# Feed-forward in three blocks of 768 tokens, its split weight operands all made during the sweeps; projection weights split once

## The chip, the cores and the metric

The kernel runs on one core of a Trainium2 chip. The metric is the device time of one launch in microseconds. A core has five engines that run side by side and meet at semaphores: TensorE (PE, with its weight loads as PEld), VectorE (DVE), ScalarE (ACT), GpSimd (POOL), and SyncE (SP), which issues most of the DMA transfers. Each engine takes its instructions strictly in the order in which they stand in its queue.

## The reference, cut to what matters

There are 2304 tokens (2048 of `x_sample`, 256 of `x_prompt`), each a vector of 1024 numbers, and one layer.

```
h = rmsnorm(x, norm1_g);  p = h @ w_in                      # 1024 -> 2336
a_out = gla_mixer(q, k, v, g, lr, ...)                      # gated linear attention, both directions
b_out = spatial_gating(gelu(u), gelu(vs), ...)              # 128 x 128 mixing of positions
c_out = pool_mixer(xp, ...)                                 # means over 2, 4, 8, 16 positions
x = x + concatenate([a_out, b_out, c_out]) @ w_o            # 1024 -> 1024
h = rmsnorm(x, norm2_g)
a, up = split(h @ w_ffn_in)                                 # 1024 -> 2 x 2816
a = conv of width 3 over the tokens, per channel
x = x + (silu(a) * up) @ w_ffn_out                          # 2816 -> 1024
y = rmsnorm(x, norm_f)
```

All arrays are float32. The kernel gets float32 accuracy from a faster format of matmul by splitting each operand into a high part (the number rounded to that format) and a low part (what is left), and adding three products: high x high, high x low, low x high. So each product costs three matmuls, and each operand must be split once on ACT (the high part, a copy that rounds) and on DVE or POOL (the low part, a subtraction).

## The kernel before

The program has three stages.

**Sweep 1** goes once over the 18 tiles of 128 tokens: `main1` multiplies a tile by 1312 columns of `w_in`, whose split form (`wk`) stays on chip, and `post1` does the parts of the attention that need only this tile. It also prepares `w_o` (`wo_prep`): scales it, folds the pooling weights in, and writes it to DRAM (`d_w`) unsplit.

**Sweep 2** goes over the tiles again, grouped in five supers of three or four tiles (`SUPERS`). `main2` multiplies by the other 1024 columns of `w_in` (`vk`), and `gla2`, `sgu2` and `gate2` finish the three mixers into the split operand `mh`, `ml`. After each super `out2` multiplies it by `w_o`, in eight chunks of 128 output channels. Each chunk's `w_o` is loaded from `d_w` again (`wo_load`, tile `rawo` or `wr`, three chunks ahead, in the last super one) and split again (`wo_split` into `oh`, `ol`): five supers split the same `w_o` five times. The `out2` of the last super runs together with `hprep`, which makes the right-hand operands of the first feed-forward block (the seven combinations `B`).

**The feed-forward** goes over four blocks of 576 tokens, each in two halves of 288 (`CH`). For each of the 22 groups of 128 hidden channels (`NJ`), `ffn1` computes both halves and both branches with a scheme of seven products in place of eight: seven left operands (`NAMES`: A11, S2, S1, S3, S4, A12, A22, made of sums and differences of quarters of `w_ffn_in`), each with one of the seven operands B, four steps of 128 channels and three matmuls each: 84 matmuls of 290 columns (288 and a halo of one on either side). `gate` then does the convolution, SiLU and the product, and splits the result into `uh`, `ul`. The hidden groups come in parts (`PARTS`, 4+3+3+4+4+4); after each part `ffn2` multiplies by `w_ffn_out`, loaded three jobs ahead (`rg`) and split (`gh`, `gl`), and adds to the output tile `x2` (48 matmuls per hidden group and block).

The left operands are made in the first block alone: `operands` (L1049 to L1107) loads a group of `w_ffn_in` (`rawa`, `rawu`), forms the sums on POOL (`comb`, L1041, tiles `sr`), splits seven operands of 128 x 512 on ACT with DVE or POOL (`op`, tiles named after `NAMES`), and stores each, 512 KB, to DRAM (`d_a`). The other three blocks load them from there into a ring of `NAO` = 10 buffers.

**What sets the order.** PE's order is that of the code. The other engines are ordered by a scheduler in sweep 1 and by the code from the second tile of sweep 2 on (`MAN`). Side work is written as generators in a `Pipe`: it advances by one tick after every group of three matmuls, and a generator says after how many ticks its next piece is issued. So the piece's place in each engine's queue is fixed in counts of PE's work, not in time.

Of the kernel before, what the change touches and what calls it, by code (L numbers as in the profile page):

```python
# [45 lines left out]
FG = (11, 3, 6, 13, 5, 2)  # L46
# [6 lines left out]
HL = (2, 2)  # L53
# [66 lines left out]
def trunk(ctx: ExitStack, tc: tile.TileContext, xT, wa, wb, gw2, gb, rows, wsT, plw, wo, w1, w2, vec, cst, yT):  # L120
# [15 lines left out]
    def rawt(name):  # L136
        return rawp.tile([P, 1024], F32, tag="raw", name=name)
# [5 lines left out]
    d_w = [dr.tile([P, KD, P], F32, name=f"dw{c}") for c in range(KD)]  # L143
# [35 lines left out]
    pipe, hpipe, opipe, hjobs = Pipe(), Pipe(), Pipe(), []  # L179
# [6 lines left out]

    xpool = pool("xpool", 2)
    if True:
        w1p = pool("s1w", 1)
# [127 lines left out]
        def post1(i, p1):  # L317
# [142 lines left out]
        def wo_prep(c):  # L460
# [11 lines left out]
            GP.dma_start(out=d_w[c], in_=rv)  # L472

        for i in range(NT):
# [16 lines left out]

    if True:
# [134 lines left out]
        def main2(i, n, get, t0):  # L627
# [5 lines left out]
            def mm(k, g):  # L633
# [22 lines left out]
        def wo_load(u, c, a):  # L656
            if u == len(SUPERS) - 1:
                rv = box2["acc"].tile([P, 4, P], F32, tag="wr", name="wr", bufs=2)
            else:
                if a == 0:  # L660
                    wx["raw", c] = rawt("rawo").rearrange("p (k n) -> p k n", k=KD)
                rv = wx["raw", c][:, 4 * a:4 * a + 4]
            wx["raw", c, a] = rv
            SY.dma_start(out=rv, in_=d_w[c][:, 4 * a:4 * a + 4])

        def wo_split(c, a):
            if a == 0:
                wx["h"] = box2["o"].tile([P, KD, P], F32R, tag="oh", name="oh")
                wx["l"] = box2["o"].tile([P, KD, P], F32R, tag="ol", name="ol")
            split(wx["h"][:, 4 * a:4 * a + 4], wx["l"][:, 4 * a:4 * a + 4], wx.pop(("raw", c, a)))  # L670
# [63 lines left out]
        def look(u):  # L734
            return 1 if u == len(SUPERS) - 1 else 3

        def ahead2(u):

            for c in range(look(u)):
                for a in range(2):  # L740
                    wo_load(u, c, a)
# [1 line left out]
            yield 8
            for a in range(2):
                wo_split(0, a)
                wo_load(u, look(u), a)
                yield 2
# [706 lines left out]
```

## Time and profile before

| | us |
|---|---|
| median of 3 runs | 2545.81 (2545.32 to 2547.29) |
| the profiled execution | 2544.5 |
| its span, first to last instruction | 2542.7 |
| PE busy | 2439.0 (96%) |
| DVE busy | 1575.0 (62%) |
| ACT busy | 920.5 (36%) |
| POOL busy | 546.5 (21%) |
| DMA moved | 570.96 MB, mean 225 GB/s |

A busy time is the union of an engine's instructions. The profile models the ends of matmuls, so PE's 96% does not say that PE runs at its peak; how fast it goes is read from how many matmuls begin in a stretch. Between the median and the profiled span lie 3.1 us: 1.8 us outside the first and last instruction, and 1.3 us by which the profiled execution was below the median.

### The profile page before, as it was taken

Reading aid. Unit: us, or ns where it says so; the run is one execution under the profiler, and the core shown is the slowest. Engines: PE = TensorE matmul, PEld = TensorE weight load, DVE = VectorE, ACT = ScalarE, POOL = GpSimd, SP = SyncE. Lnnn points to the kernel's source line nnn. Section 1 sums busy time; section 2 is a strip of 40 time slices with the busy share of each in tenths; the row PEclk is TensorE's granted clock in tenths of the full one; section 3 lists DMA queues with packets and bytes.
Section 4 is the critical chain, followed back from the end, with each engine's and each line's share of the span. In section 5 each row is a group of like instructions: output and inputs, shape, how many; then the busy total and the mean of one; then the engine's idle time right before and its main releaser. Section 6 shows DMA issues by size and latency. Waiting matters only on the chain.

```text
span 2542.7 us, 43323 instructions
## 1 busy us (share of the span) xinstructions
PE 2439.0 (96%) x16334; PEld 2321.1 (91%) x16334; DVE 1575.0 (62%) x3185; ACT 920.5 (36%) x1814; POOL 546.5 (21%) x586
## 2 busy tenths in 40 slices
PE   8999998999999889999998999999999999899998
PEld 7999997998887789989998999999999999899997
DVE  6655547667656887887665555565455446455455
ACT  6444444333333544444342222242222224122224
POOL 3332221001002754566340000030000004000001
PEclk9999999999999999999999999999999999999999
DMA  6332214566555796999687888679688867677664
GB/s 204 121 125 108 75 71 147 166 202 184 158 164 162 277 357 238 288 337 292 250 261 277 244 295 250 243 270 326 241 258 294 266 235 263 243 249 250 228 227 137
DMA packets 261747, 570.96 MB, mean 225 GB/s; under 512 B 33858, under 2 KB 122050, under 8 KB 261540
## 3 DMA queue, kind: packets, MB, share of 16 engines
q1 hardware_dynamic: 254516, 545.36, 64.1%
q0 software_dynamic: 6752, 22.55, 2.3%
q8 instruction: 129, 2.11, 0.3%
q14 instruction: 78, 0.64, 0.1%
q10 hardware_dynamic: 272, 0.29, 0.0%
HBM read 430.30 MB, written 137.81 MB: 223 GB/s over the span
## 4 chain that ended last, share of the span: by engine, by line
PE 47%; DMA 9%; DVE 4%; issue 3%; POOL 2%; SPq 1%; ACT 1%; DVEq 0%; ACTq 0%; POOLq 0%
PE py L175 6%; PE py L174 6%; PE py L173 6%; DMA rg<-in_w 4%; PE fB L1130 3%; PE fB L1129 3%; PE fB L1131 3%; PE fA L1130 3%; PE fD L1129 3%; PE fA L1131 3%; PE fA L1129 3%; PE fD L1130 3%; PE fD L1131 3%; DMA out_y<-x 1%; PE fC L1130 1%
## 5 line engine op out<-in xcount | busy, mean ns | idle before, releaser
L173 PE MATMUL py<-uh,gh 128*128 128x288 f32 (+1 forms) x1408 | 422.3, 300 | 14.2 <-ACT gh L1197 14.2
L175 PE MATMUL py<-uh,gl 128*128 128x288 f32 (+1 forms) x1408 | 422.5, 300 | 5.1 <-DVE gl L1199 4.8
L174 PE MATMUL py<-ul,gh 128*128 128x288 f32 (+1 forms) x1408 | 421.2, 299 | 2.8 <-DVE ul L1162 2.8
L173 PEld LDWEIGHTS py<-uh,gh 128*128 128x128 f32 x1408 | 270.4, 192 | 16.8 <-ACT gh L1197 16.5
L175 PEld LDWEIGHTS py<-uh,gl 128*128 128x128 f32 x1408 | 269.4, 191 | 9.0 <-DVE gl L1199 8.9
L1244 DVE TENSOR_TENSOR x<-py,x 128x288 f32<-128x288 f32 (+1 forms) x384 | 173.9, 456 | 165.6 <-PE py L175 162.0
L174 PEld LDWEIGHTS py<-ul,gh 128*128 128x128 f32 x1408 | 269.6, 191 | 4.6 <-DVE ul L1162 4.2
L1197 ACT ACTIVATE gh<-rg 128x512 fp32r<-128x512 f32 (+1 forms) x198 | 117.7, 595 | 362.9 <-PE py L174 192.6
L1129 PE MATMUL fB<-B,S 128*128 128x290 f32 (+1 forms) x704 | 211.2, 300 | 12.9 <-DVE e L1141 12.9
L1130 PE MATMUL fB<-B,S 128*128 128x290 f32 (+1 forms) x704 | 210.1, 298 | 0.0
L1131 PE MATMUL fB<-B,S 128*128 128x290 f32 (+1 forms) x704 | 209.2, 297 | 0.0
L1130 PE MATMUL fA<-B,A 128*128 128x290 f32 (+1 forms) x704 | 209.2, 297 | 0.0
L1131 PE MATMUL fA<-B,A 128*128 128x290 f32 (+1 forms) x704 | 208.8, 297 | 0.0
L1129 PE MATMUL fA<-B,A 128*128 128x290 f32 (+1 forms) x704 | 208.6, 296 | 0.0
L1199 DVE TENSOR_TENSOR gl<-rg,gh 128x512 fp32r<-128x512 f32 (+1 forms) x198 | 143.2, 723 | 92.9 <-ACT gh L1197 88.0
L1141 DVE TENSOR_TENSOR e<-fB,e 128x290 f32<-128x290 f32 (+1 forms) x176 | 80.6, 458 | 167.8 <-PE fB L1131 154.3
L1149 ACT ACTIVATE t<-e,vc 128x288 f32<-128x288 f32 (+1 forms) x88 | 55.4, 629 | 332.1 <-DVE e L1141 332.1
L173 PE MATMUL pm<-wk,xh 128*128 128x512 f32 (+2 forms) x432 | 166.8, 386 | 6.0 <-ACT wk L168 6.0
L174 PE MATMUL pm<-wk,xh 128*128 128x512 f32 (+2 forms) x432 | 157.5, 365 | 0.4 <-DVE wk L169 0.2
L175 PE MATMUL pm<-wk,xl 128*128 128x512 f32 (+2 forms) x432 | 156.8, 363 | 0.4 <-DVE xl L166 0.4
L1129 PEld LDWEIGHTS fB<-B,S 128*128 128x128 f32 x704 | 133.7, 190 | 15.4 <-DVE e L1141 15.3
L1129 PE MATMUL fD<-B,A 128*128 128x290 f32 (+1 forms) x352 | 107.9, 306 | 30.0 <-DVE u L1141 30.0
(272 smaller groups left out, 6497.7 us busy)
## 6 DMA issues: line engine op xcount, KB each, us to landing
S<-da_S SPq DMA_DIRECT2D x264, 512.0 KB, 5.2
A<-da_A SPq DMA_DIRECT2D x198, 512.0 KB, 5.2
da_S<-S SPq DMA_DIRECT2D x88, 512.0 KB, 7.6
rg<-in_w SPq DMA_DIRECT2D x134, 256.0 KB, 6.1
da_A<-A SPq DMA_DIRECT2D x66, 512.0 KB, 8.2
xt<-in_xT SPq DMA_DIRECT2D x35, 512.0 KB, 4.0
rawo<-dw SPq DMA_DIRECT2D x64, 256.0 KB, 4.1
rg<-in_w SPq DMA_DIRECT2D x64, 192.0 KB, 5.9
```

What stands on the lines that cost most here:

```text
L173: TE.matmul(out, lh, rhs_h, start=first, stop=False)
L174: TE.matmul(out, lh, rhs_l, start=False, stop=False)
L175: TE.matmul(out, ll, rhs_h, start=False, stop=last)
L1129: TE.matmul(o, ah, bh, start=st, stop=False, skip_group_check=True)
L1130: TE.matmul(o, ah, bl, start=False, stop=False, skip_group_check=True)
L1131: TE.matmul(o, al, bh, start=False, stop=kk == 3, skip_group_check=True)
L1141: V.tensor_tensor(out=out, in0=a, in1=b, op=ALU.add)
L1149: SC.activation(t0, a[:, 1:1 + no], AF.Identity, scale=cw(1), bias=vc[:, V_CB + j:V_CB + j + 1])
L1197: SC.activation(gh[:, 0:n], rv, AF.Copy)
L1199: V.tensor_tensor(out=gl[:, 0:n], in0=rv, in1=gh[:, 0:n].bitcast(F32), op=ALU.subtract)
L1244: V.tensor_tensor(out=x2[:, c, 1:1 + no], in0=py[q][:, 0:no], in1=x2[:, c, 1:1 + no], op=ALU.add)
```

## The change

**Blocks.** `CH` goes from 288 to 384: three blocks of 768 tokens in halves of 384, in place of four of 576 in halves of 288. Matmuls of `ffn1` have 386 columns (388 in the last block), those of `ffn2` 384 (386). There are 8712 of them in place of 11616. `PARTS` has eight parts (3,3,3,3,3,2,2,3) in place of six, `NAO` is 7 in place of 10, and the ticks at which the end of a block is finished (`FG`) and the next one's operands are loaded (`HL`) are other numbers.

**Left operands.** `operands` only loads now, in every block. The making of the operands moves to a new generator `wprep`, with its own pipe `wpipe`: ten of the 22 groups in sweep 1 and twelve in sweep 2 (from the third tile on, over the tiles and the `out2` of the first four supers). It works in halves of 256 columns, takes every low part on POOL, and stores each half, 256 KB, from SP.

**`w_o`.** `wo_prep` splits it once and stores both parts (`d_w` doubles). `wo_split` is gone; `wo_load` brings the split halves, 512 KB each, into four buffers, two chunks ahead.

```
-NAO = 10
+NAO = 7
-FG = (11, 3, 6, 13, 5, 2)
+FG = (6, 3, 4, 8, 2, 1)
-HL = (2, 2)
+HL = (1, 2)
-PARTS = (4, 3, 3, 4, 4, 4)
+PARTS = (3, 3, 3, 3, 3, 2, 2, 3)
-CH = 288
+CH = 384
-SUPERS = (((13, 3),), ((10, 3),), ((6, 4),), ((2, 4),), ((0, 2), (16, 2)))
+SUPERS = (((13, 3),), ((9, 4),), ((6, 3),), ((2, 4),), ((0, 2), (16, 2)))
...
+    def wprep(js, raws, work, gaps):
+        load, half = gaps
+        def store(j, n, k, t):
+            yield 2
+            SY.dma_start(out=d_a[j][NAMES.index(n)][:, :, k:k + 2], in_=t.bitcast(F32))
+        for j in js:
+            ra, ru = (raws(n).rearrange("p (k n) -> p k n", k=KD) for n in ("rawa", "rawu"))
+            SY.dma_start(out=ra, in_=w1[j][:, 0])
+            SY.dma_start(out=ru, in_=w1[j][:, 1])
+            yield load
+            tt = work.tile([P, 4, P], F32, tag="wt", name="wt", bufs=1)
+            a11, a12, a21, a22 = ra[:, 0:4], ra[:, 4:8], ru[:, 0:4], ru[:, 4:8]
+            for n, dst, a, b, o in (("A11", a11, None, None, None), ("S3", tt, a11, a21, ALU.subtract), ("S1", a21, a21, a22, ALU.add),
+                                    ("A22", a22, None, None, None), ("S2", a11, a21, a11, ALU.subtract),
+                                    ("S4", tt, a12, a11, ALU.subtract), ("A12", a12, None, None, None)):
+                if o is not None:
+                    GP.tensor_tensor(out=dst, in0=a, in1=b, op=o)
+                    yield 1
+                for k in (0, 2):
+                    t = work.tile([P, 2, 2, P], F32R, tag="wo", name="wo")
+                    split(t[:, 0], t[:, 1], dst[:, k:k + 2], eng=GP)
+                    begin(wpipe, store(j, n, k, t))
+                    yield half
...
             SC.activation(raw[:, 6 * P:8 * P], pf[:, 0:2 * P], AF.Copy)
-            GP.dma_start(out=d_w[c], in_=rv)
+            hi = rawt("rawh", F32R)
+            split(hi, raw.bitcast(F32R), raw)
+            GP.dma_start(out=d_w[c][:, 0], in_=hi.bitcast(F32).rearrange("p (k n) -> p k n", k=KD))
+            GP.dma_start(out=d_w[c][:, 1], in_=rv)
...
+        wpipe.add(wprep(range(NFIRST), lambda n: wk1.tile([P, 1024], F32, tag=n, name=n, bufs=1), wk1, (8, 2)), 30)
...
+        def wo_load(c, a):
+            wx[c, a] = t = box2["o"].tile([P, 2, 4, P], F32R, tag="ow", name="ow", bufs=4)
+            SY.dma_start(out=t.bitcast(F32), in_=d_w[c][:, :, 4 * a:4 * a + 4])
...
-                    if c + 1 < KD and k in (2, 4):
-                        wo_split(c + 1, k // 2 - 1)
-                        if c + 1 + look(u) < KD:
-                            wo_load(u, c + 1 + look(u), k // 2 - 1)
+                    if c and k == 1 and c + 1 < KD:
+                        wo_load(c + 1, 1)
+                    if k == 5 and c + 2 < KD:
+                        wo_load(c + 2, 0)
...
+                    box2["wk"] = pool("wk2", 4, "right")
+                    wpipe.add(wprep(range(NFIRST, NJ), rawt, box2["wk"], (10, 2)))
...
         def operands():
-            ...
-            for i in range(NJ, len(BLOCKS) * NJ):
+            for i in range(len(BLOCKS) * NJ):
                 A = fw[i] = {}
                 for e, n in enumerate(NAMES):
-                    SY.dma_start(out=take(A, n).bitcast(F32), in_=d_a[i % NJ][e])
+                    A[n] = fa.tile([P, 2, 4, P], F32R, tag="ao", name=n, bufs=NAO)
+                    SY.dma_start(out=A[n].bitcast(F32), in_=d_a[i % NJ][e])
                     yield
```

The order of the instructions shows the moves at three places.

POOL in sweep 1, one tile's worth of rows, before: `sq` and `rr` are the tile's sum of squares and its inverse root (which ACT needs to empty the tile's sums), the DMA rows are stores of the attention's parts.

```order
L217 TENSOR_TENSOR sq<-sq 128x512
L271 TENSOR_TENSOR rr<-ms,mhalf 128x1
L218 TENSOR_TENSOR sq<-sq 128x256
L272 TENSOR_SCALAR rh<-rr 128x1
L219 TENSOR_TENSOR sq<-sq 128x128
L381 DMA dq_72<-qT 128x512
L395 DMA de_107<-sx 128x512
```

The same place in the changed kernel; `wo` is a half of a left operand, `wt` a difference of two quarters.

```order
L249 TENSOR_TENSOR sq<-sq 128x512
L302 TENSOR_TENSOR rr<-ms,mhalf 128x1
L250 TENSOR_TENSOR sq<-sq 128x256
L303 TENSOR_SCALAR rh<-rr 128x1
L251 TENSOR_TENSOR sq<-sq 128x128
L413 DMA dq_69<-qT 128x512
L427 DMA de_104<-sx 128x512
L203 TENSOR_TENSOR wt<-rawa,rawu 128x512
L166 TENSOR_TENSOR wo<-rawa,wo 128x256
L203 TENSOR_TENSOR rawu<-rawu 128x512
L166 TENSOR_TENSOR wo<-rawa,wo 128x256
```

POOL now has 14 subtractions `wo` and four sums or differences per group between the tile's own work.

SP in the `out2` of the first super, before: per chunk the raw `w_o` (two halves of 256 KB), a strip of x (`xr`) and the store of the sum (`dx`).

```order
L664 DMA rawo<-dw_143 128x512 x2
L664 DMA rawo<-dw_144 128x512 x2
L676 DMA xr<-in_xT 128x3x128
L728 DMA dx_148<-xr 128x384
L664 DMA rawo<-dw_145 128x512 x2
L676 DMA xr<-in_xT 128x3x128
L728 DMA dx_148<-xr 128x384
```

In the changed kernel the same stretch holds the split `w_o` (`ow`, halves of 512 KB), and the raw loads and stores of `wprep`.

```order
L698 DMA ow<-dw_139 128x2x512
L190 DMA da_A_220<-wo 256x1x256
L194 DMA rawa<-in_w 128x1024
L195 DMA rawu<-in_w 128x1024
L190 DMA da_A_220<-wo 256x1x256
L698 DMA ow<-dw_140 128x2x512
L704 DMA xr<-in_xT 128x3x128
L756 DMA dx_299<-xr 128x384
L698 DMA ow<-dw_140 128x2x512
L698 DMA ow<-dw_141 128x2x512
L704 DMA xr<-in_xT 128x3x128
L190 DMA da_A_222<-wo 256x1x256
```

From the fifth load of `ow` to the last store of `dx` SP issues transfers of 15680 KB in this `out2`, and of 17600, 17344 and 17664 KB in the next three (rows counted, shapes multiplied out).

DVE in the first feed-forward block, one hidden group, before: `e` and `u` empty PE's sums, `A` and `S` are low parts of left operands.

```order
L1141 TENSOR_TENSOR e_8593<-fC,e_8616 128x290
L166 TENSOR_TENSOR A_8642<-rawa,A_8642 128x512
L1141 TENSOR_TENSOR u_8657<-fD,e_8593 128x290
L166 TENSOR_TENSOR A_8662<-rawu,A_8662 128x512
L1141 TENSOR_TENSOR e_8593<-fB,e_8593 128x290
L166 TENSOR_TENSOR A_8685<-rawa,A_8685 128x512
L1151 SCALAR_TENSOR_TENSOR t_8692<-e_8593,vc,t_8692 128x288
```

And now:

```order
L1095 TENSOR_TENSOR e_9940<-fC,e_9957 128x386
L1095 TENSOR_TENSOR u_9992<-fD,e_9940 128x386
L1095 TENSOR_TENSOR e_9940<-fB,e_9940 128x386
L1105 SCALAR_TENSOR_TENSOR t_10017<-e_9940,vc,t_10017 128x384
L1106 SCALAR_TENSOR_TENSOR t_10017<-e_9940,vc,t_10017 128x384
```

The subtractions that stood between the emptying steps are gone; each step is a third wider.

## Rows read from the trace of the kernel before

**Rows 1.** The page's part 1.

```profile
PE 2439.0 (96%) x16334; PEld 2321.1 (91%) x16334; DVE 1575.0 (62%) x3185; ACT 920.5 (36%) x1814; POOL 546.5 (21%) x586
```

**Rows 2.** Stretches: us, engines' busy time (instructions), PE clock, DMA share, GB/s.

```profile
6.00:387.20 381.20, 379.20 (x2316) 347.08 (x2316) 224.07 (x451) 184.80 (x334) 113.11 (x198) 1.00 0.32 115
...
458.00:491.40 33.40, 33.40 (x194) 33.40 (x193) 18.07 (x37) 11.26 (x26) 0.00 (x0) 1.00 0.49 160
491.40:532.60 41.20, 41.20 (x218) 34.99 (x218) 31.09 (x84) 15.77 (x27) 8.54 (x7) 1.00 0.58 175
532.60:566.30 33.70, 33.70 (x196) 33.67 (x195) 20.93 (x44) 11.71 (x28) 0.00 (x0) 1.00 0.69 211
...
719.60:763.20 43.60, 43.60 (x194) 36.09 (x193) 20.58 (x38) 12.00 (x26) 0.00 (x0) 1.00 0.49 156
...
804.90:867.20 62.30, 51.89 (x202) 37.92 (x202) 48.91 (x69) 27.71 (x67) 36.35 (x34) 0.95 0.75 252
867.20:1305.10 437.90, 403.78 (x2917) 396.75 (x2917) 347.59 (x545) 194.04 (x389) 248.65 (x179) 0.98 0.84 291
1305.10:1714.70 409.60, 397.02 (x2926) 394.33 (x2925) 224.06 (x476) 120.08 (x252) 38.40 (x37) 0.99 0.81 264
1714.70:2122.20 407.50, 395.98 (x2926) 393.09 (x2926) 224.33 (x476) 119.79 (x251) 39.43 (x57) 0.99 0.79 266
2122.20:2527.50 405.30, 398.43 (x2931) 396.50 (x2929) 216.85 (x465) 119.21 (x247) 13.98 (x20) 0.99 0.67 233
```

**Rows 3.** The same columns, two stretches inside the last feed-forward block.

```profile
2200.00:2250.00 50.00, 50.00 (x375) 50.00 (x374) 22.91 (x49) 11.24 (x22) 0.00 (x0) 1.00 0.62 216
2250.00:2300.00 50.00, 50.00 (x373) 50.00 (x373) 26.89 (x60) 13.41 (x28) 0.00 (x0) 1.00 0.66 228
```

**Rows 4.** PE's waits in the first block: us in total, times, longest.

```profile
PE fB L1129 <- DVE e L1141: 12.9, 10, 1.7
PE fD L1129 <- DVE u L1141: 10.2, 6, 3.5
```

**Rows 5.** The same view in the second block (1305.1 to 1714.7 us).

```profile
PE fD L1129 <- DVE u L1141: 7.0, 2, 5.6
```

**Rows 6.** SP's issue of that wait's load: start, us, what.

```profile
1356.11 1.77 SPq L1190 DMA_DIRECT2D rg<-in_w  x2
```

**Rows 7.** ACT behind it.

```profile
1366.15 1.30 ACT L1197 ACTIVATE gh<-rg 128x512 fp32r<-128x512 f32 x2 [10.72 <-DMA rg<-in_w]
```

**Rows 8.** PE's waits in the last super's `out2` (804.9 to 867.2 us).

```profile
PE pw L173 <- ACT oh L165: 7.0, 3, 2.9
```

**Rows 9.** Groups of POOL, shapes apart: busy us, mean ns | idle before.

```profile
L1044 POOL TENSOR_TENSOR sr<-rawu 128x512 f32<-128x512 f32 x22 | 35.2, 1602 | 6.7 <-DMA rawu<-in_w 6.7
...
L218 POOL TENSOR_TENSOR sq<-sq 128x256 f32<-128x256 f32 x18 | 14.5, 804 | 0.3
```

**Rows 10.** Groups of DVE, shapes apart.

```profile
L166 DVE TENSOR_TENSOR A<-rawa,A 128x512 fp32r<-128x512 f32 x44 | 62.0, 1410 | 1.6 <-ACT A L165 1.6
...
L166 DVE TENSOR_TENSOR ol<-rawo,oh 128x512 fp32r<-128x512 f32 x64 | 43.9, 691 | 25.1 <-ACT oh L165 22.7 <-DMA xr<-in_xT 1.0
```

**Rows 11.** A step of one tile's attention in sweep 1, on DVE.

```profile
239.05 0.69 DVE L166 TENSOR_TENSOR lal<-la,lah 128x512 fp32r<-128x512 f32 x1 [0.70 <-ACT lah L165]
```

**Rows 12.** PE, which takes it up.

```profile
240.07 0.28 PE L353 MATMUL pg<-lah,tri 128*128 128x256 f32 x1
240.19 0.28 PE L353 MATMUL pg<-lal,tri 128*128 128x256 f32 x1
```

**Rows 13.** The stretch in which DMA moved most: columns as in Rows 2.

```profile
890.00:910.00 20.00, 18.34 (x136) 18.11 (x135) 19.50 (x27) 9.88 (x20) 15.36 (x10) 1.00 1.03 416
```

**Rows 14.** DMA issues: line, count, KB each, median us to landing.

```profile
da_S<-S SPq DMA_DIRECT2D x88, 512.0 KB, 7.6
```

More of the change, by code (lines that the diff above doesn't have):

```diff
@@ L134, in pmt, with rawt @@
         return psp.tile([P, 512], F32, tag="pm", name=name, bufs=3)
-    def rawt(name):
-        return rawp.tile([P, 1024], F32, tag="raw", name=name)
+    def rawt(name, dt=F32):
+        return rawp.tile([P, 1024], dt, tag="raw", name=name)
     d_q = [dr.tile([P, 512], F32, name=f"dq{i}") for i in range(NT)]
@@ L142, in trunk @@
     d_c = [dr.tile([P, 2, 2, P], F32, name=f"dc{i}") for i in range(NT)]
-    d_w = [dr.tile([P, KD, P], F32, name=f"dw{c}") for c in range(KD)]
+    d_w = [dr.tile([P, 2, KD, P], F32, name=f"dw{c}") for c in range(KD)]
+    d_a = [[dr.tile([P, 2, 4, P], F32, name=f"da{j}_{n}") for n in NAMES] for j in range(NJ)]
     tiles_of = [[i for s, n in runs for i in range(s, s + n)] for runs in SUPERS]
@@ L178, in trunk, with begin @@
     v4 = lambda t_: t_.rearrange("p (h e d) -> p h e d", h=4, e=2)
-    pipe, hpipe, opipe, hjobs = Pipe(), Pipe(), Pipe(), []
+    pipe, hpipe, opipe, wpipe, hjobs = Pipe(), Pipe(), Pipe(), Pipe(), []
+    def begin(to, gen):
+        to.add(gen, next(gen))
+    def wprep(js, raws, work, gaps):
[21 more added lines that the diff above has]
+                    yield half
     SC.preload_act_table_set("natural_log_exp_and_others")
@@ L257, in trunk @@
         NZ = 2
-        af = [sp.tile([P, 512], F32, name=f"af{i}", bufs=1) for i in range(NZ)]
-        ab = [sp.tile([P, 512], F32, name=f"ab{i}", bufs=1) for i in range(NZ)]
-        for t_ in af + ab:
+        a0, a1 = (sp.tile([P, 512], F32, name=n, bufs=1) for n in ("af", "ab"))
+        for t_ in (a0, a1):
             GP.memset(t_, 0.0)
@@ L488, in trunk @@
                 end1 = main1([i])
+        wpipe.flush()
+        wk1.release()
         w1p.release()
@@ L654, in main2 @@
                 pipe.add(pool2(i, get, t0), hold(6))
[L656 to L670, printed above, removed]
+        def wo_load(c, a):
+            wx[c, a] = t = box2["o"].tile([P, 2, 4, P], F32R, tag="ow", name="ow", bufs=4)
+            SY.dma_start(out=t.bitcast(F32), in_=d_w[c][:, :, 4 * a:4 * a + 4])
         def xr_load(u, c):
@@ L732, in trunk @@
         wx = {}
-        def look(u):
-            return 1 if u == len(SUPERS) - 1 else 3
         def ahead2(u):
-            for c in range(look(u)):
+            for c in range(2):
                 for a in range(2):
-                    wo_load(u, c, a)
+                    wo_load(c, a)
             wx[0] = xr_load(u, 0)
[L743 to L747, printed above, removed]
+            return
+            yield
         def out2(u, get, between=None, begun=None):
@@ L765, in out2 @@
             for c in range(KD):
-                oh, ol, xr = wx.pop("h"), wx.pop("l"), wx.pop(c)
+                ow, xr = [wx.pop((c, a)) for a in range(2)], wx.pop(c)
                 pw_ = pmt("pw") if c or not begun else begun
@@ L857, in trunk @@
         xpool.release()
+        rawp.release()
     if True:
@@ L876, in atmp @@
             return ft.tile([P, CW], F32, tag="sq", name=name, bufs=2)
-        def begin(gen):
-            pipe.add(gen, next(gen))
         def cols_of(segs):
@@ L1132, in prod @@
                     if kk == 0:
-                        if fast and a in ("A12", "A22"):
-                            pipe.add(lead(1, 0), 12)
-                        else:
-                            astep()
+                        astep()
                     pipe.tick()
@@ L1291, in starts_of @@
         def starts_of(no):
-            return list(range(0, no - P + 1, P)) + [no - P]
+            return list(range(0, no - P + 1, P)) + [no - P] * (no % P > 0)
         def last_norm(blk, q, xs, no, acc):
@@ L1344, in trunk @@
             no = box["w"] - 2
-            nbox = {"wait": 34}
+            nbox = {"wait": 30}
             for q, n in enumerate(PARTS):
```

99 lines of the change are left out of this document (23 added, 76 removed).

## The prediction

> **What bounds the kernel now.** I read the page's part 1 first: PE is busy for 96% of the span [rows 1], so other engines matter only where they make PE wait. Since a busy share hides short waits, I next cut the span into stages (the view by stretches) and counted matmuls [rows 2, 3]. In undisturbed feed-forward, two stretches of 50 us hold 375 and 373 matmuls; each stretch counts about two that reach over its edges, so 100 us hold 744, one every 134.4 ns [rows 3]. A block has 22 x (84 + 48) = 2904 matmuls, which at that pace take 390.3 us. The four blocks took 437.9, 409.6, 407.5 and 405.3 us [rows 2], so they lost 47.6, 19.3, 17.2 and 15.0 us, 99 in all; their sum is 1660.3.
>
> Third, I looked for what the loss waits for. In the first block PE waits for DVE to empty its sums [rows 4], and DVE is busy 347.6 of 437.9 us there against 224 later [rows 2]: it takes low parts of left operands at 1410 ns each [rows 10]. In the second block one wait of 5.6 us stands out [rows 5]: a load of `w_ffn_out` issued at 1356.1 us reached ACT only at 1366.2 [rows 6, 7], and the subtraction behind it held DVE, which was to empty PE's sums. So block 1 is short of DVE, POOL and DMA together, and the later ones lose mostly at their start, where transfers crowd. In the sweeps PE waits little: ACT, DVE and POOL have room, and DMA is at 0.32 in sweep 1 and 0.49 to 0.69 in sweep 2 [rows 2]. The last `out2` takes 62.3 us for the 192 matmuls that take 43.6 elsewhere [rows 2], and waits for the splits of `w_o` [rows 8].
>
> **Wider blocks.** The same sums are made by fewer, wider matmuls. What one costs at 384 columns is in the trace: 192 of them took 33.4 us, 174.0 ns each; at 512, 192 took 43.6 us, 227.1 ns [rows 2]. From 289 over 384 to 512 that is a straight line of 0.416 ns a column with about 14 ns that do not depend on the width. Before: 11616 x 134.4 ns = 1561.2 us. After: 5544 of 386 columns at 174.8 ns and 3168 of 384 at 174.0 make 1520.3 us. Gain 40.9, and I see nothing that could take it: weight loads per matmul stay the same, and each has longer to hide.
>
> **Losses inside the blocks.** The first block no longer makes operands: 88 splits of 512 columns with 88 sums leave ACT, DVE and POOL, so its 47.6 us should fall to those of a later block. One block start falls away. Operands now arrive at 3.67 MB per hidden group in 84 x 174.8 ns = 14.7 us (250 GB/s) in place of 11.3 us (325 GB/s), so the crowding at a start eases. New are two more parts per block and a ring of 7 buffers: six products ahead, 12 x 174.8 x 6 = 12.6 us, where a transfer of that size took 7.6 us to land in the crowded block [rows 14]. I take losses of 15, 13 and 12 us; the ends are 7 each (if the starts become clean) and 20 each (the worst of a later block now). 99 - 40 = 59 gained, between 39 and 78.
>
> **Last `out2`.** Without `wo_split` the waits of 7.0 us go [rows 8]; all above 43.6 us is 18.7. The making of `B` beside it gets a third wider, and the six first operands are loaded. I take 12.
>
> **Sweep 1 gets ten hidden groups.** Each adds to POOL 14 subtractions of 256 columns (nearest row 804 ns) and four sums of 512 (1602 ns) [rows 9]: 17.7 us, 177 in all on 113.1 of 381.2 us [rows 2], 76%. It fits. What it costs is order: a subtraction of DVE with both inputs in SBUF took 691 ns where POOL was quiet and 1410 where POOL was at work [rows 10], so steps of the attention end up to 0.72 us later, while PE takes up `lal`, ready at 239.74, at 240.19: 0.45 us of slack [rows 11, 12]. Nothing is the low end; four such steps per tile (`lal`, `qd`, `kd`, `at`) late without any slack are 4 x 0.72 x 18 = 52 us, the high end. I take 0.45 us a tile, 8 us, since the other three steps have more slack. Here the page "SBUF — State Buffer" of the Trainium skill, section "Who interferes with whom", says that a DVE instruction with two SBUF inputs and a POOL instruction that reads SBUF exclude each other for a whole instruction; the doubled 691 agrees. By that rule a late step costs a whole POOL subtraction, 0.8 us in place of 0.72, and the 52 would be 58.
>
> **Sweep 2 gets twelve, and `w_o` in twice the bytes.** `wo_split` leaves (64 of DVE's 691 ns lie beside PE's work [rows 10]), so DVE and ACT come out about even, and POOL has room. The price is DMA. In the four `out2` with `wprep` SP issues 15680 + 17600 + 17344 + 17664 KB, 69.9 MB, by the order of the changed kernel, in a time in which PE needs 2 x 33.4 + 2 x 43.6 = 154.0 us [rows 2]: 454 GB/s. The most that the trace shows is 416 GB/s, in 20 us [rows 13]; sweep 2's own mix of small pieces made 211 GB/s at a share of 0.69, 306 for a full share [rows 2]. So 168 to 229 us are needed, 14 to 75 over PE's. PE must wait, for `ow` comes only two chunks ahead through the same queue. The new bytes are longer pieces than the old mix but shorter than those of the 416; I take 350, 200 us, 46 over. Between, `main2` has 175 GB/s [rows 2] and 16 of a group's 42 ticks per tile, 0.38 x 4.72 MB in 13.7 us or 131 GB/s: 306 together, just what the lower end carries, so nothing there. The page "DMA: Bandwidth & Descriptors" of the Trainium skill, section "Where 436 GB/s comes from", names about 358 GB/s as what binds a core's transfers from and to HBM and 435 as the fabric's ceiling. The trace went beyond the first [rows 13]; by 358 the four `out2` would need 195 us, 41 over, and by 435 161 us, 7 over.
>
> **Sum.** 2544.5 (the profiled execution; its span and 1.8 us around it) - 41 - 59 - 12 + 8 + 46 = 2486.5. The median of the runs was 1.3 above the profiled one: 2488.
>
> **The rivals.**
> (a) DMA has room. The four `out2` run at the 416 of [rows 13] and lose 14: 2456. For it: packets of 1 KB and more, one queue. Against: sweep 2 never came near that rate.
> (b) Slower: the sweeps give back more than the blocks gain. The place is DVE's steps in the tiles' chains: if POOL's subtractions delay four steps a tile by 0.72 us in both sweeps (36 tiles, 104 us) and DMA gives only the 306 (75 us), the sweeps lose 179 against 112 gained: 2613. It decides from 112 us of loss in the sweeps on. For it: POOL at 76%, DVE's doubled subtraction [rows 10], a slack of 0.45 us. Against: other steps may have more slack, and PE's order stays.
> (c) The change does not do what it says: the blocks do not get cleaner, because the shorter ring runs dry at each of the 24 starts of a part. At 2 us each (a third of the 5.6 of [rows 5]) that is 48 more: 2536. Against: 12.6 us of lead over a landing of 7.6.
>
> **How the numbers follow.** Forecast 0.52, (a) 0.25, (b) 0.15, (c) 0.08. The forecast's own range is 2460 to 2520. The range for 8 in 10 is 2435 to 2555: below it lies (a) with clean blocks as well (losses of 21, 19 less than taken), above it most of (b). A measurement can tell a change of about 0.2%, 5 us. Faster are the forecast, (a) and half of (c), 0.81; within 5 us 0.03, from (c) and the mild end of (b); slower 0.16.
>
> **What would show it.** Right: in undisturbed feed-forward about 286 matmuls per 50 us; a first block of about 522 us and no longer than the others by more than a few us; no low parts of left operands on DVE there; `out2` of the first four supers together near 200 us in place of 154, with a DMA share near 1 and PE waiting for DMA of `ow`; sweep 1 near 389 us. Wrong: `out2` at PE's pace (then (a)); waits of PE for DVE in every tile of the sweeps (then (b)); PE waiting for DMA of left operands in the blocks (then (c)).

## The result, and the profile after

The changed kernel takes 2688.9 us (2685.6 to 2693.4, 4 runs) against 2546.6 us (4 runs): a ratio of 1.056, interval 1.0542 to 1.0579. It is 5.6% slower, where 2488 us had been forecast. The profiled execution, from which the stages below are read, took 2693.4 us, 4.5 above the median.

The page's part 1, PE's row, and from part 2 the granted clock in 40 slices of the span (9 is 90% or more):

```profile
PE 2495.0 (93%) x13416; PEld 2350.8 (87%) x13416; DVE 1453.1 (54%) x2693; ACT 844.0 (31%) x1702; POOL 650.5 (24%) x798
...
PEclk9888989989998999999999999999999999999998
```

PE has 2918 instructions fewer than in [rows 1] and yet is busy for longer. But for the last slice, the clock is below 90% only in the first 13 of 40 slices; the sweeps end after 16.

The stretches that answer to [rows 2]: sweep 1, `out2` of the first four supers, the last `out2`, the three blocks (same columns):

```profile
6.60:491.10 484.50, 422.75 (x2316) 377.15 (x2316) 281.17 (x459) 237.87 (x482) 279.20 (x386) 0.91 0.58 197
568.00:626.20 58.20, 41.54 (x193) 38.32 (x192) 11.99 (x22) 13.05 (x37) 24.46 (x30) 0.88 0.93 309
691.00:753.00 62.00, 50.41 (x196) 38.50 (x195) 19.39 (x33) 14.12 (x39) 23.99 (x28) 0.92 0.97 325
804.40:861.50 57.10, 41.15 (x194) 38.16 (x193) 16.87 (x31) 14.79 (x41) 28.23 (x33) 0.88 1.02 340
929.30:985.90 56.60, 48.85 (x194) 37.54 (x193) 15.56 (x24) 14.13 (x38) 26.54 (x31) 0.94 0.99 334
1035.00:1092.30 57.30, 50.07 (x203) 38.96 (x203) 32.68 (x50) 19.05 (x45) 27.15 (x26) 0.94 0.86 285
1092.30:1615.70 523.40, 517.49 (x2917) 515.17 (x2917) 279.32 (x510) 136.37 (x262) 39.70 (x33) 0.99 0.65 212
1615.70:2145.80 530.10, 521.60 (x2926) 517.49 (x2925) 286.94 (x524) 138.81 (x269) 46.95 (x56) 0.99 0.66 214
2145.80:2672.80 527.00, 521.73 (x2932) 519.26 (x2930) 272.11 (x510) 135.31 (x263) 17.70 (x21) 0.99 0.57 183
```

The feed-forward gains 80 us (1660 to 1580). The sweeps lose 230: sweep 1 103, `main2` 47, the four `out2` 80; the last `out2` gains 5. Sweep 1 does the same 2316 matmuls, but PE is busy for 422.8 us in place of 379.2 at a clock of 0.91 in place of 1.00, and idle for 61.8 in place of 2.0. So 43.6 us of the 103 are PE's longer busy time on the same matmuls, and 60 are waits. Weighted with the clock granted at each moment (the trace's clock records), the 422.8 us are 385.1 us at full clock: about 38 of the 43.6 us are the lower clock, and the other 6 are left open.

What PE waits for in sweep 1 (60 to 400 us; total, times, longest; where the kernel before showed 0.5 us for `lal` and nothing else of the attention):

```profile
PE pg L385 <- ACT lah L165: 18.1, 8, 3.7
PE ptq L406 <- DVE qd L397: 16.5, 4, 6.3
PE pz L370 <- DVE lrs L363: 5.9, 6, 1.6
PE pg L385 <- DVE lal L166: 5.0, 9, 1.2
```

They are steps of the tiles' attention, late by up to 6.3 us at once. The lines alone leave open whether DVE, ACT or a queue makes them late. In the four `out2` PE waits for hardly anything but the loads of `ow`; here the first of them:

```profile
PE pw L173 <- DMA ow<-dw: 16.3, 9, 4.1
```

### The profile page after: what moved, and what is told of

The parts are those of the page before. It is cut to its first block, busy times and chain, and to the rows that moved or that the text cites. A ratio compares the mean times of both kernels' runs of the same rounds, so it can differ in the third digit from the quotient of the medians.

```text
span 2691.6 us, 37292 instructions
## 1 busy us (share of the span) xinstructions
PE 2495.0 (93%) x13416; PEld 2350.8 (87%) x13416; DVE 1453.1 (54%) x2693; ACT 844.0 (31%) x1702; POOL 650.5 (24%) x798
## 4 chain that ended last, share of the span: by engine, by line
PE 63%; DMA 14%; POOL 8%; issue 6%; DVE 5%; ACT 2%; SPq 2%; POOLq 0%; ACTq 0%; DVEq 0%
PE py L174 6%; PE py L175 6%; PE py L173 6%; DMA da_S<-wo 4%; PE fB L1086 3%; PE fB L1088 3%; PE fA L1086 3%; PE fB L1087 3%; PE fD L1088 3%; PE fA L1088 3%; PE fD L1086 3%; PE fD L1087 3%; PE fA L1087 3%; POOL wo L166 2%; DMA dx<-xr 2%
## 5 line engine op out<-in xcount | busy, mean ns | idle before, releaser
L173 PE MATMUL py<-uh,gh 128*128 128x384 f32 (+1 forms) x1056 | 358.8, 340 | 4.2 <-ACT gh L1151 4.2
L174 PE MATMUL py<-ul,gh 128*128 128x384 f32 (+1 forms) x1056 | 358.2, 339 | 1.3 <-DVE ul L1116 1.3
L175 PE MATMUL py<-uh,gl 128*128 128x384 f32 (+1 forms) x1056 | 357.9, 339 | 1.2 <-DVE gl L1153 1.2
L1198 DVE TENSOR_TENSOR x<-py,x 128x384 f32<-128x384 f32 (+1 forms) x384 | 213.6, 558 | 179.9 <-PE py L175 175.1
L1095 DVE TENSOR_TENSOR e<-fB,e 128x386 f32<-128x386 f32 (+1 forms) x132 | 74.0, 560 | 269.3 <-PE fB L1088 258.9
L173 PEld LDWEIGHTS py<-uh,gh 128*128 128x128 f32 x1056 | 199.6, 189 | 5.3 <-ACT gh L1151 4.9
L1151 ACT ACTIVATE gh<-rg 128x384 fp32r<-128x384 f32 (+1 forms) x198 | 97.7, 498 | 334.1 <-PE py L174 244.8
L1086 PE MATMUL fB<-B,S 128*128 128x386 f32 (+1 forms) x528 | 180.1, 341 | 7.3 <-DMA S<-da_S 7.3
L173 PE MATMUL pw<-mh,ow 128*128 128x512 f32 (+1 forms) x320 | 131.2, 410 | 58.8 <-DMA ow<-dw 57.8
L1086 PE MATMUL fA<-B,A 128*128 128x386 f32 (+1 forms) x528 | 181.1, 343 | 0.2 <-DMA A<-da_A 0.2
L1088 PE MATMUL fB<-B,S 128*128 128x386 f32 (+1 forms) x528 | 179.9, 341 | 0.0
L1088 PE MATMUL fA<-B,A 128*128 128x386 f32 (+1 forms) x528 | 179.7, 340 | 0.0
L1087 PE MATMUL fA<-B,A 128*128 128x386 f32 (+1 forms) x528 | 179.3, 340 | 0.0
L1087 PE MATMUL fB<-B,S 128*128 128x386 f32 (+1 forms) x528 | 179.2, 339 | 0.0
```

The source lines that it names most:

```text
L173: TE.matmul(out, lh, rhs_h, start=first, stop=False)
L174: TE.matmul(out, lh, rhs_l, start=False, stop=False)
L175: TE.matmul(out, ll, rhs_h, start=False, stop=last)
L1086: TE.matmul(o, ah, bh, start=st, stop=False, skip_group_check=True)
L1087: TE.matmul(o, ah, bl, start=False, stop=False, skip_group_check=True)
L1088: TE.matmul(o, al, bh, start=False, stop=kk == 3, skip_group_check=True)
```

## The experiments

All kernels start from the changed one. Stage times, in us, run from the first to the last matmul of a stage in each trace; `main2` is the sum of its five pieces, `out2` of its four with making beside them.

| kernel | sweep 1 | main2 | four out2 | last out2 | feed-forward | ratio to before (95%) |
|---|---|---|---|---|---|---|
| before | 381 | 263 | 155 | 62 | 1660 | 1 |
| changed | 484 | 310 | 234 | 57 | 1580 | 1.056 (1.0542 to 1.0579) |
| no making | 384 | 265 | 171 | 55 | 1578 | 0.977 (0.9757 to 0.9789) |
| no stores | 502 | 298 | 184 | 56 | 1580 | 1.043 (1.0407 to 1.0443) |
| low parts on DVE | 437 | 315 | 233 | 55 | 1572 | 1.037 (1.0353 to 1.0390) |
| stores issued by POOL | 524 | 336 | 216 | 55 | 1572 | 1.074 (1.0727 to 1.0759) |
| ACT's part alone | 397 | 267 | 183 | 56 | 1585 | 0.987 (0.9828 to 0.9920) |
| POOL's part alone | 499 | 300 | 184 | 57 | 1581 | 1.040 (1.0360 to 1.0432) |
| half of w_o | 483 | 312 | 203 | 50 | 1574 | 1.043 (1.0386 to 1.0468) |
| memsets on POOL | 398 | 277 | 182 | 59 | 1582 | 0.993 (0.9909 to 0.9955) |
| all on DVE | 421 | 299 | 235 | 57 | 1574 | 1.027 (1.0243 to 1.0287) |
| made in block 1 | 386 | 264 | 176 | 60 | 1682 | 1.018 (1.0162 to 1.0195) |
| made evenly | 383 | 264 | 174 | 57 | 1652 | 1.003 (1.0017 to 1.0044) |
| gl on POOL too | 385 | 263 | 174 | 57 | 1654 | 1.004 (1.0026 to 1.0057) |

**1. No making** (2485.0 us).

```
-wpipe.add(wprep(...))                       # in both sweeps
-SY.dma_start(out=A[n].bitcast(F32), in_=d_a[i % NJ][e])
+SY.dma_start(out=A[n].bitcast(F32), in_=d_w[i % KD][:, e % 2] ...)
```

> Left out: the left operands are not made; the feed-forward loads as many bytes of w_o's split form in their place. All theories expect the sweeps to lose what the making put on them: sweep 1 back from 484.5 to 381-392 us, main2 from 309 to about 265, the four out2 from 234 to 154-175 (w_o still comes in twice the bytes), so about 2688 - 104 - 47 - 70 = 2467 us. If sweep 1 stays above 400, the loss there comes from something other than the making (the split of w_o, the pools' new places). It prices the making as a whole and shows what the blocks alone are worth.

The stages came as expected; the total lies 18 us above the 2467. Sweep 1 in one row:

```profile
7.30:391.10 383.80, 379.32 (x2316) 346.89 (x2316) 231.77 (x459) 192.96 (x342) 115.23 (x206) 1.00 0.34 125
```

The making costs 101 us in sweep 1, 45 in `main2` and 64 in `out2`. The doubled bytes of `w_o` by themselves cost 16 in `out2`, and the feed-forward takes what it takes with real operands. So the changed kernel without the making would be 2.3% faster than before; that is what the wide blocks could give at most.

**2. No stores** (2652.0 us). My first theory R was that stores make it: ACT's copies wait for a buffer until its store has landed.

```
-begin(wpipe, store(j, n, k, t))             # and d_w in place of d_a, as in 1
```

> Left out: the made operands are not stored; the feed-forward loads as many bytes of w_o's split form in their place; loads, splits and sums of the making stay. Theory R (ring): ACT's splits stand ahead of the tiles' steps in its queue and wait for one of three buffers until its store has landed, and SP, which issues the store, stands waiting for POOL's subtraction; so without stores sweep 1 falls to 395-425 us from 484.5, and the four out2 from 234 to 155-175 (some 22 of 70 MB gone). Rival D (DVE slowed by POOL's subtractions) and rival W (the added work of ACT and POOL itself) expect sweep 1 at 460 or more, since all compute stays.

R fell. Sweep 1 does not shrink to 395-425, it grows to 502, with the DMA share down from 0.58 to 0.33. So taking the stores away gains PE nothing in sweep 1. For `out2` they are 51 of the 80 us; at 184 us it stays above the 155 to 175 that were expected without them.

**3. Low parts on DVE** (2638.5 us).

```
-split(t[:, 0], t[:, 1], dst[:, k:k + 2], eng=GP)
+split(t[:, 0], t[:, 1], dst[:, k:k + 2])
```

> The low parts of the left operands go from POOL to DVE in both sweeps. Rival D (POOL's subtractions slow DVE's steps, which PE waits for): sweep 1 falls from 484.5 to about 400-420, since POOL keeps 4 sums per group only. Theory R (ACT waits for a buffer until its store has landed): the subtraction ends sooner, so stores go out somewhat earlier: 450-475. Rival W (the work as such): no gain, or a loss, since DVE now carries more: 480-510.

Sweep 1 at 437: below what R and W allowed, above D's 400-420. Taking 100 us of work off POOL in sweep 1 (279 to 178 us busy) and giving 37 to DVE gains 47 us there; in `main2` it gains nothing.

**4. Stores issued by POOL** (2732.7 us).

```
-SY.dma_start(out=d_a[j][NAMES.index(n)][:, :, k:k + 2], in_=t.bitcast(F32))
+GP.dma_start(out=d_a[j][NAMES.index(n)][:, :, k:k + 2], in_=t.bitcast(F32))
```

> The stores of the made operands are issued by POOL, right behind its own subtraction's place, and no longer by SP, which then waits for no subtraction. Theory R in the form that SP's wait for POOL makes stores and the loads behind them late: sweep 1 falls from 484.5 to 430-460 and ACT's wait for a raw load all but goes. If the buffer's wait for landing alone counts, or D or W holds: 475-500, and POOL's issues add to its load (280 issues at 1 us or more).

Worse than any theory gave: sweep 1 is 524, POOL busy 378 us. Taking SP's waits for POOL's subtractions away (180 us between 60 and 400 us in the changed kernel) gained nothing in sweep 1. It does not price them, though: POOL got 140 issues more there, of 0.75 us each. More work on POOL costs PE more.

**5 and 6. ACT's part alone, POOL's part alone** (2512.0 and 2644.8 us).

```
 # 5: no GP.tensor_tensor, no store, in place of the split:
+SC.activation(t[:, 0], dst[:, k:k + 2], AF.Copy)
 # 6: the four sums stay, no store, in place of the split:
+GP.tensor_tensor(out=t[:, 1], in0=dst[:, k:k + 2], in1=a22[:, k:k + 2], op=ALU.subtract)
```

> Left out: of the making only the raw loads and ACT's 14 copies per group stay, with no sum or subtraction on POOL and no store; the feed-forward loads as many bytes of w_o's split form. Without stores sweep 1 took 502 us, so the loss there is in the engines' work, not in DMA. Theory C (coupling: ACT's copy waits in its queue for a buffer that POOL's subtraction holds, and the tile's steps behind it come late): 385-400, as ACT waits for nothing but raw loads. Rival D (DVE stretched by POOL) and rival Q (the tile's own steps on POOL queue behind the subtractions): 385-395 too. Rival W (ACT's added work itself): 430 or more.

> Left out: of the making only the raw loads and POOL's 4 sums and 14 subtractions per group stay (the subtraction takes another raw piece in place of ACT's copy), with no copy on ACT and no store; the feed-forward loads as many bytes of w_o's split form. Theory C (coupling through ACT's queue): 385-405, as ACT no longer stands behind POOL. Rivals D (DVE's steps stretched by POOL) and Q (the tile's steps queued on POOL): 430-480.

ACT's copies and the raw loads cost sweep 1 13 us, POOL's part alone 115, more than the whole making (101) and more than the 430 to 480 us allowed for. So neither ACT's added work (W) nor the coupling through ACT's queue (C) is needed for the loss. Whether C adds to it in the changed kernel, these two runs do not tell. Sweep 1 with POOL's part alone:

```profile
6.10:505.00 498.90, 413.97 (x2316) 373.53 (x2316) 287.25 (x459) 193.06 (x342) 279.90 (x386) 0.89 0.33 118
```

DVE has the same 459 instructions as without making, in nearly the same order (444 of 458 keep it, by names), but is busy for 287.3 us in place of 231.8. PE has 34.7 us more of busy time and 80.4 more of idle.

**7. Half of w_o** (2652.7 us).

```
-tile([P, 2, 4, P], F32R, tag="ow", ...);  in_=d_w[c][:, :, 4 * a:4 * a + 4]
+tile([P, 1, 4, P], F32R, tag="ow", ...);  in_=d_w[c][:, 0:1, 4 * a:4 * a + 4]
```

> Left out: the low part of w_o, whose place PE gives to the high part; out2 loads 256 KB per half chunk in place of 512, as many bytes as unsplit w_o would be, 4.2 of some 17 MB less in each of the four out2 with making. If DMA's rate bounds out2 there: at the 327 GB/s that the four had, 53 MB take 163 us, so 234 falls to 165-185. If the making's splits or the queue of SP bound it, it stays above 210. Sweep 1 and the feed-forward as in the changed kernel.

In between: 203. The first of the four:

```profile
562.20:611.40 49.20, 39.38 (x194) 36.62 (x194) 11.46 (x22) 12.59 (x36) 24.00 (x29) 0.90 0.85 270
```

Fewer bytes make `out2` faster, so DMA's bytes do set the pace, but at a share of 0.85 to 0.92 no longer all the time; PE still waits for `ow` (9.8 us here), whose load stands in one queue with stores and raw loads. What bounds it at that share was not tried.

**8. Memsets on POOL** (2528.7 us): does it matter that POOL is occupied, or that it reads?

```
-GP.tensor_tensor(out=dst, in0=a, in1=b, op=o)
+GP.memset(ra, 0.0)
-split(t[:, 0], t[:, 1], dst[:, k:k + 2], eng=GP)
+GP.memset((ru, ra)[k // 2][:, 0:7], 0.0)
```

> Left out: the making is replaced by raw loads and 18 memsets per group on POOL (14 of 896 columns, 4 of 1024), which hold POOL for about the 16.7 us that its sums and subtractions of a group took, but read nothing from SBUF; no ACT copies, no stores; the feed-forward loads as many bytes of w_o's split form. POOL's sums and subtractions alone made sweep 1 499 us. Theory D (DVE's steps are stretched while POOL reads SBUF): 385-400. Rival Q (the tile's own steps on POOL - the inverse root, the copies of xp, the stores - stand queued behind the making): 470-510.

```profile
6.60:404.30 397.70, 387.41 (x2316) 352.57 (x2316) 233.55 (x459) 193.03 (x342) 263.17 (x386) 0.98 0.42 147
```

POOL is held for 263 us, nearly as long as in 6 (148 us of it by memsets, where the subtractions and sums took 165), and sweep 1 takes 398 in place of 499. So rival Q (the tile's own steps queue on POOL) is not enough: POOL held, without reading, costs 14 us and not 115. D stands as the main cause. DVE's groups, shapes apart, 60 to 400 us: first with memsets,

```profile
L166 DVE TENSOR_TENSOR xl<-xt,xh 128x1024 fp32r<-128x1024 f32 x14 | 17.1, 1223 | 6.9 <-ACT xh L165 6.8
L437 DVE TENSOR_TENSOR at<-af,ab 128x512 f32<-128x512 f32 x17 | 12.8, 755 | 0.6
...
L395 DVE SCALAR_TENSOR_TENSOR qd<-p,qd 128x256 f32<-128x256 f32 x32 | 12.1, 419 | 1.0 <-ACT qd L390 1.0
...
L410 DVE COPY kT<-ptk 128x512 f32<-128x512 f32 x17 | 11.7, 690 | 26.6 <-PE ptk L406 26.5
...
L397 DVE TENSOR_TENSOR kd<-p,kd 128x512 f32<-128x512 f32 x16 | 10.9, 684 | 0.0
...
L427 DVE TENSOR_TENSOR sx<-pu,sx 64x512 f32<-64x512 f32 x14 | 9.5, 682 | 1.1
```

then with POOL's part alone,

```profile
L396 DVE SCALAR_TENSOR_TENSOR qd<-p,qd 128x256 f32<-128x256 f32 x24 | 15.8, 696 | 0.4 <-ACT qd L391 0.2
L398 DVE TENSOR_TENSOR kd<-p,kd 128x512 f32<-128x512 f32 x12 | 14.9, 1245 | 0.0
L166 DVE TENSOR_TENSOR xl<-xt,xh 128x1024 fp32r<-128x1024 f32 x10 | 14.3, 1431 | 3.2 <-ACT xh L165 3.2
...
L411 DVE COPY kT<-ptk 128x512 f32<-128x512 f32 x12 | 8.3, 688 | 14.6 <-PE ptk L407 14.5
L428 DVE TENSOR_TENSOR sx<-pu,sx 64x512 f32<-64x512 f32 x11 | 7.5, 682 | 0.8
```

and in the changed kernel:

```profile
L166 DVE TENSOR_TENSOR xl<-xt,xh 128x1024 fp32r<-128x1024 f32 x11 | 23.1, 2101 | 10.4 <-ACT xh L165 6.9 <-DMA da_A<-wo 3.5
L397 DVE SCALAR_TENSOR_TENSOR qd<-p,qd 128x256 f32<-128x256 f32 x26 | 17.3, 703 | 0.6 <-ACT qd L392 0.6
L439 DVE TENSOR_TENSOR at<-af,ab 128x512 f32<-128x512 f32 x13 | 15.5, 1194 | 0.4
...
L412 DVE COPY kT<-ptk 128x512 f32<-128x512 f32 x13 | 9.0, 690 | 14.3 <-PE ptk L408 14.2
```

With memsets these steps take what they take without making. Beside POOL's subtractions the steps whose inputs both lie in SBUF take up to 1.8 times as long, though not each of them in each kernel: `xl`, `qd` and `kd` in 6, `xl`, `qd` and `at` in the changed kernel, where `kd` takes 720 ns. Those with an input in PSUM (`kT`, `sx<-pu`) stay within 2 ns of 690 and 682. The Trainium skill's page "SBUF — State Buffer", section "Who interferes with whom", says that a DVE instruction with two SBUF inputs contends with a POOL instruction that reads SBUF, and not with one that only writes it; these rows of sweep 1 agree (`kd` 1245 ns beside subtractions, 684 beside memsets).

How such a step reaches PE is seen in the changed kernel. Three of them follow each other on DVE, and PE stands behind the third:

```profile
111.95 3.59 DVE L496 TENSOR_TENSOR rawo<-rawo,vc 128x1024 f32<-128x1024 f32 x1 [4.01 <-DMA rawo<-in_wo]
115.47 2.28 DVE L166 TENSOR_TENSOR xl<-xt,xh 128x1024 fp32r<-128x1024 f32 x1
117.67 2.88 DVE L397 SCALAR_TENSOR_TENSOR qd<-p,qd 128x256 f32<-128x256 f32 x2
...
120.70 1.09 PE L406 MATMUL ptq<-cs,qd 128*128 128x128 f32 x4 [6.34 <-DVE qd L397]
```

They take 8.8 us; by their means without making it would be 3.3. But D is not the only way. In 6 PE's longest wait stands behind DVE's wait for `xp`, a copy of the tile's own that queues on POOL behind the making (which there stood 6.6 us for its raw load), so Q has its part there:

```profile
119.53 4.13 DVE L468 TENSOR_TENSOR s<-xp 128x286 f32<-128x286 f32 x1 [10.55 <-POOL xp L455]
123.69 3.13 DVE L469 TENSOR_TENSOR s<-s 128x282 f32<-128x282 f32 x1
...
129.16 1.19 PE L434 MATMUL pa<-qT,kT 64*128 64x128 f32 x4 [17.18 <-DVE kT L411]
```

And in the changed kernel some waits for `lah`, PE's largest group of waits, come through ACT's queue, where a copy of the making waits for its raw load and `e`, `la` and `lah` of the tile stand behind it (C):

```profile
191.54 0.73 ACT L165 ACTIVATE wo<-rawa 128x256 fp32r<-128x256 f32 x2 [5.77 <-DMA rawa<-in_w]
...
196.94 0.58 PE L385 MATMUL pg<-lah,tri 128*128 128x256 f32 x1 [3.68 <-ACT lah L165]
```

How the loss of sweep 1 divides between these ways was not measured. One reservation: in sweep 1 a scheduler places the steps of DVE and ACT, and it placed some neighbours otherwise in 6 than in 8 (431 of 458 DVE instructions keep their order), with PE's order the same. In `main2` the order is that of the code; there 6 takes 300 us and 8 takes 277. PE's wait is for one step, `vn`; first 6, then 8 (all of sweep 2; total, times, longest):

```profile
PE pb L618 <- DVE vn L614: 24.6, 11, 4.7
...
PE pb L617 <- DVE vn L613: 7.9, 7, 2.5
```

In the changed kernel this wait is 26.8 us, without making there is none. So in `main2`, with the order fixed, a POOL that writes without reading costs 12 of some 35 us, and the reading work the rest.

**9. All on DVE** (2613.5 us).

```
-GP.tensor_tensor(out=dst, in0=a, in1=b, op=o)
+V.tensor_tensor(out=dst, in0=a, in1=b, op=o)         # and the low parts, as in 3
```

> Complete computation; low parts and sums of the making go from POOL to DVE, in both sweeps. Per group DVE gets 14 x 0.42 + 4 x 0.69 = 8.6 us, 86 us in sweep 1 beside the 224 that it had there. If POOL's presence is what costs (D or Q alike), sweep 1 falls from 437 (low parts on DVE) to 395-420, with main2 falling from 309 to about 280 and the four out2 staying at 220-235, bound by DMA: total 2580-2620. If it is the amount of added work that costs, sweep 1 stays at 437 or more.

Sweep 1 at 421, just outside the 395-420; `out2` at 235 and the total as expected; `main2` fell by 10 only, to 299 where about 280 was expected. ACT's copies, the stores and the raw loads are all still there, and with 82 us more of work on DVE than without making they cost sweep 1 37 us; with the low parts and sums on POOL it was 101. So most of the loss there hangs on POOL's part, by this run too. The same work on DVE costs less, but it is not free.

**10 to 12. Can the wide blocks be kept?** Sweeps without making, operands made in block 1 from quarters of `w_ffn_in`; shorter parts make room. In 11, among other things, one operand is made every 6 groups of three matmuls, with the sums on DVE; in 12 the low part `gl` of `w_ffn_out` is POOL's in block 1.

```
+for i in range(NJ):                         # 10; op() splits into the ring and stores to d_a
+    op("A11", a11); sub(tt, a11, a21); sub(a21, a21, a22, ALU.add); sub(a11, a21, a11)
+    yield; op("S2", a11); yield; op("S1", a21, GP); yield; op("S3", tt, GP); ...
-PARTS = (3, 3, 3, 3, 3, 2, 2, 3)
+PARTS = (2,) * 9 + (1, 3)
+sub(tt, a11, a21); sub(a11, a22, tt)        # 11: S2 two sums deep, on DVE
+(GP if made["n"] < 7 * NJ else V).tensor_tensor(out=gl[:, 0:n], ...)      # 12
```

> Complete computation; the three wide blocks stay, but the left operands are made in the first block, from quarters of w_ffn_in (256 KB each) loaded as their buffers come free, low parts on DVE (A11, S2, A12, A22) and POOL (S1, S3, S4), the sums on POOL; to make room the parts are of two hidden groups (the last of three). Without any making the kernel took 2485 us; making in the first of four narrow blocks cost 47.6 - 17 = 31 us, and wide blocks leave more time per group: 2505-2540, first block 545-575, sweep 1 384-390. If the short ring (6 ahead, where it was 9) or POOL's sums make PE wait at every hidden group (2 us x 22), 2550-2580.

2591.7 us, above both ranges: block 1 took 605.3, and the other blocks, with the short parts, 10 to 13 us more than without making. Where ACT waited in block 1:

```profile
ACT S L165 <- POOL a L1088: 102.3, 20, 6.3
ACT S L165 <- POOL wt L1088: 65.4, 20, 3.5
```

In 20 of the 22 groups ACT's copy of S2 waited for the last of three sums on POOL, up to 6.3 us.

> Complete computation. As the kernel whose operands are made in block 1, where ACT waited 102 us for POOL's sums (copy of S2) and block 1 took 605 us: now one operand is made every 6 groups of three matmuls, through the second products too, the sums are on DVE (S2 as a22 - S3, two sums deep in place of three), low parts of S1, S3, A22 on POOL, A22 used and freed before A12, and the high part of the next w_ffn_out comes a tick earlier. If ACT's wait for the sums was what made block 1 long: 535-560 us there, total 2530-2555. If loads landing late or DVE's load are what counts: 580 or more, total 2570 and up. Against the kernel before (about 2545) either way within 1%, and so a test of the cause more than a gain.

2557.0 us, block 1 574.0. Block 1 fell by 31, so that cause was right in the main, though several things were changed at once, and 2 us more than expected remain in the total and 14 in block 1. What is left there:

```profile
PE py L177 <- DVE gl L1232: 29.4, 24, 2.3
```

> Complete computation. As the kernel whose operands are made evenly over block 1 (2557 us, block 1 574.0), where PE waited 29.4 us in 24 waits for the low part of w_ffn_out (gl) on DVE and once 8 us for a sum behind loads of the second hidden group: in block 1 gl goes to POOL, and the first operand of the second group is made 16 ticks after the one before. If DVE's queue in the second products is what is left: block 1 at 540-555, total 2525-2542, faster than the kernel before (about 2546). If POOL's added subtractions stretch DVE's steps as they did in sweep 1, block 1 stays at 565-590 and the total at 2550-2575.

```profile
PE py L177 <- POOL gl L1232: 26.3, 15, 4.1
```

2556.5 us, block 1 578.0: the wait moved from DVE to POOL, and the total and block 1 lie where the rival had them. No complete version beats the kernel before; the best is 0.3% behind it. In 11 the making in block 1 costs 49 us there (574.0 against 524.6 without making), and the later blocks, with the short parts that give it room, take another 25; in the sweeps it cost 210.

## Why the prediction was wrong

Measured against the terms of the sum, from the profiled executions:

| term | forecast | measured |
|---|---|---|
| wider matmuls | -41 | -27 |
| losses inside the blocks | -59 | -53 |
| last `out2` | -12 | -5 |
| sweep 1 | +8 | +103 |
| four `out2` | +46 | +80 |
| `main2` | 0 | +47 |
| the end of the program | 0 | +4 |
| sum | -58 | +149 |

**The step that failed** is "I take 0.45 us a tile, 8 us, since the other three steps have more slack", and with it the high end of 52. The mechanism was in the text, the doubled subtraction of [rows 10], but I put it down to four steps a tile at 0.72 us each, minus a slack; the slack was read for `lal` alone, and for that of the other three no row stands there. The runs show three things in its place. First, the lateness adds up along the tile: DVE's 459 instructions took 55.5 us more (experiment 6 against 1), the steps behind them on ACT, POOL and DVE queue up, and PE stood for up to 6.3 us at once, not 0.7. Second, PE's waits came with a lower granted clock, 0.91 on the mean of sweep 1 between its two levels of 1.2 and 2.4 GHz, and about 38 of the 103 us are matmuls at that clock. No term of the sum had that. Third, I excluded `main2` ("so nothing there") because I weighed only DMA for it; steps with two SBUF inputs are stretched there too (`vn<-vn,rw` 1054 ns in one stretch of 6, 425 in the same place of 8), and the order by code shows their part: 300 us with POOL's subtractions, 277 with memsets, 265 with neither.

**Rival (b)** named place and mechanism: DVE's steps late through POOL. Its 104 us were meant for 36 tiles; sweep 1's 18 alone gave 115 (experiment 6). It had a chance of 0.15 because I judged each step's slack singly. Its 2613 was still 76 us short of the result, and it had neither the clock nor the queues.

**Four `out2`.** That DMA is short and PE waits for `ow` was right. Two sizes were off. At a full share the four stretches moved 332, 335, 333 and 337 GB/s (309 over 0.93 and so on), where I took 350. And they moved 76.4 MB (rate times time, summed), not 69.9: that count begins at the fifth load of `ow`, while by the trace SP issues 73.5 MB in the four stretches, and the rest had been issued before they began. 76.4 MB at 334 GB/s are 229 us; measured are 234. The stores make 51 of the 80, the raw loads and copies 13, the doubled `w_o` 16.

**Wider matmuls.** I took 174.8 and 174.0 ns from one `out2` stretch of 192 matmuls. Undisturbed feed-forward now:

```profile
1400.00:1450.00 50.00, 50.00 (x286) 49.99 (x285) 26.77 (x50) 13.90 (x26) 0.00 (x0) 1.00 0.81 253
1450.00:1500.00 50.00, 50.00 (x286) 49.99 (x285) 25.82 (x50) 10.75 (x22) 0.00 (x0) 1.00 0.49 161
```

Counted as in [rows 3] that is 568 in 100 us, 176.1 ns; 8712 of them take 1534 us, 27 less than before. The 286 that I had named is there by count, but it is a count with its edges.

**Losses inside the blocks.** By that pace a block needs 511.4 us, so they lost 12.0, 18.7 and 15.6, where I had 15, 13 and 12. Right in kind: the first block is now the shortest. Rival (c), a ring that runs dry, did not happen: PE waited for a left operand once in block 1 (2.7 us), and in the others for 4.0 and 3.3 us, some 60 us after their start.

**Last `out2`.** The waits for the splits went; waits for `ow` at a DMA share of 0.86 came.

## What to carry to other kernels

An engine that is busy for 21% of the kernel and 30% of sweep 1 [rows 1, 2] is not free room: before work moves to POOL, look at which of DVE's steps on the path read both inputs from SBUF, and at which of the path's own steps queue on POOL, and price a chain of them, not each against its own slack. Price a wait of PE together with the clock at which it goes on after it. And before work moves out of a stage, ask what its making cost there: in the narrow first block it had cost about 31 us (its loss beyond that of the later blocks), and in the sweeps it cost 210.

## What the hardware showed that I had not expected

- Many short waits of PE went with a lower clock over a whole stage: in sweep 1 a granted clock of 0.91 (changed) and 0.89 (experiment 6), 1.00 without making, on the same matmuls.
- Memsets on POOL left most of DVE's two-input steps of sweep 1 alone (`sx<-sx,cc` took 784 ns in place of 692), but in `main2` single steps grew by the time of one to two and a half memsets of 0.86 us: `vn<-uv,mv`, one tensor input in SBUF, took 2.48 us in place of 0.41, `bs<-uv` 1.19 in place of 0.42, and `ml<-ptg,mh`, one input in PSUM, 1.99 in place of 0.69. Why there and not in sweep 1 was not settled.
- Taking the stores away made sweep 1 17 us longer (502 against 484). Perhaps they space POOL's subtractions out; that was not tried by itself.
